# Square sums on VectorE, the statistics' product one tick later, first FFN output unit k-major, preparation DMAs on GpSimd's queue

## The chip, the cores and the metric

The kernel runs on one core of one Trainium2 chip. The metric is the device time of one execution in microseconds (us); lower is better. PE is TensorE, DVE VectorE, ACT ScalarE, POOL GpSimd, SP SyncE; SP computes nothing here and issues DMAs. ACT and POOL issue DMAs too, each in order with its other instructions.

## What is computed

One step of a two-layer decoder on 576 tokens (512 of a prompt, 64 of samples), width 1024, fp32. Layer 0 mixes tokens with a gated MLP and differential attention, layer 1 with a diagonal state-space model (S5). Each mixer is followed by a normalised SwiGLU network. Cut to what the change touches:

```python
xp = xp + concat([a_p, b_p]) @ w_out_even[i]           # layer 0: output projection, residual
xp = xp + swiglu(rmsnorm(xp, norm_ffn[l]), w_ffn_in[l], w_ffn_out[l])
def rmsnorm(x, g): return x * lax.rsqrt(jnp.mean(x * x, axis=-1) + EPS) * g
def swiglu(h, w_in, w_out):
    gate, up = jnp.split(h @ w_in, 2, axis=-1)
    return (silu(gate) * up) @ w_out
# layer 1: S5, tables from a, dt, b, c, d only (they do not depend on x)
a_bar = jnp.exp(a * dt); b_bar = ((a_bar - 1.0) / a) * b
s = associative_scan(combine, (a_bar, b_bar @ u)) + a_cum * s0; y = Re(c @ s) + d * u
```

## The kernel before

**Layout.** The activations stay in SBUF as 8 feature blocks of 128 partitions by 576 tokens. A matrix product is cut into units: 128 output features, all tokens in two column halves of 288. fp32 precision comes from splitting each operand into a high and a low part (`hi`, `lo` for activations, `wh`, `wl` for weights) and adding three products (L278), so a unit over 8 input blocks takes 48 matmuls, one over 6 takes 36.

**The weight stream.** `Stream` holds all units in order. A `raw` tile (two units of weights) is loaded on SP's queue (L245); ACT copies it to `wh` (L260), DVE, or POOL for early units, subtracts to get `wl` (L263). `raw`, `wh` and `wl` have two buffers each, the matmuls four PSUM banks. A unit's evacuation runs on DVE. In a normal unit the first half's products over all input blocks come first, then the second half's; with `kmajor=True` the first of the two units of a push takes both halves input block by input block (`unit_mm`).

**Statistics.** `Stat` sums the squares of the residual stream over the 8 blocks: ACT squares a block (L980, L983), POOL adds it to `acc` (L991), and for the last block the square stays apart (`last`). Two sets of five tiny matmuls with a vector of ones (L1000, five column blocks of tokens) reduce `acc` and `last` over the partitions into `ssq`; twelve small DVE operations make the reciprocal root, and `bcast_rows` spreads it (`rb`). The division by the norm is applied when the FFN's first product is evacuated (L1104, L1114). There are three: `st1` after the output projection (evacuation `ev_o`, L1040), `st2` after layer 0's FFN (`ev_x2`, its products are L1518), `st3` after layer 1's mixer (`ev_z1`).

**FFN.** `push_ffn` handles the 22 blocks of hidden features in parts of 6, 6, 6 and 4: for each hidden block a gate and an up unit, then 8 output units over that part's blocks. `tu` times `tg` (L1116) gives the hidden block; ACT makes its `hi` (L227), DVE its `lo` (L228).

**S5 preparation.** Side work is split into generators; a `Driver` advances them a tick at a time between groups of matmuls. `s5_prep` builds the S5 tables during layer 0's FFN: it loads parameters (`ast`, `s0st`, `dq`, `braw`, `cst`), computes on DVE and ACT into tiles of two pools (`ablk`, 19 buffers, and `op`, 5 buffers for `Fn`, `Gn`), and stores through DRAM (`dF`, `dG`, `dZ`, `dL`, `dT`); `s5_load` loads the finished blocks back for layer 1 (`Gk`, `Fk`, `Tk`, `tabk`).

**Order.** The program is written as one sequence; a scheduler then fixes, ahead of the run, the order of instructions on every engine and DMA queue. Each engine runs its list strictly in order.

Of the kernel before, what the change touches and what calls it, by code (L numbers as in the profile page):

```python
# [77 lines left out]
def kernel(ctx, tc, I, O, stop=None, dbg=None):  # L78
# [1170 lines left out]
    def s5_prep():  # L1249
        ast = ablk("ast", (64, 4, P))  # L1250
        for c in range(2):
            A.dma_start(out=ast[:, 0, 64 * c:64 * c + 64], in_=I["ssm_a_re"][0])
            A.dma_start(out=ast[:, 1, 64 * c:64 * c + 64], in_=I["ssm_a_im"][0])
        A.dma_start(out=ast[:, 3, 0:1], in_=I["ssm_log_dt"][0].unsqueeze(1))
        V.tensor_copy(ast[:, 2, :], ast[:, 3, 0:1].to_broadcast([64, P]))
        s0st = ablk("s0st", (P, 4, P))
# [198 lines left out]
        for k in range(KD):  # L1455
# [472 lines left out]
```

## Time and profile before

| | |
|---|---|
| Median of 3 runs | 1450.46 us (1450.17 to 1450.61) |
| The profiled execution's own time | 1450.84 us |
| Its span, first to last instruction | 1449.1 us (1.7 us lie outside) |
| PE busy | 1392.5 us, 96% of the span |
| DVE, ACT, POOL busy | 829.9, 479.6, 232.8 us |
| Mean granted clock of TensorE | 0.984 |

The stages in the span: layer 0's input projection and mixers to about 340 us, its output projection to 380, its FFN to 840 (the preparation for S5 beside it), S5 to 910, layer 1's gated product and FFN from there to the end. Times of rows count from the span's start. In a row's bracket stands how long its engine was idle just before it, and what ended that.

### The profile page before, as it was taken

How to read it: one execution, taken by the hardware profiler on the slowest of the kernel's cores; microseconds unless marked ns; L12 is line 12 of the kernel's file. 1: busy time of each engine (PE TensorE's matmuls, PEld its weight loads, DVE VectorE, ACT ScalarE, POOL GpSimd, SP SyncE). 2: the span in 40 equal slices, each digit the busy share in tenths (PEclk: the TensorE clock that was granted, in tenths of full speed). 3: DMA queues.
4: the chain of work that ended last, by engine and by line, in shares of the span. 5: the costliest groups of instructions: out<-in, count | busy, mean ns of one | idle time of the engine just before them, and what ended most of it. 6: DMA issues, size and time to landing. Idle time of an engine off the chain costs nothing. (4 is left out here: it accounts for less than half of the span.)

```text
span 1449.1 us, 27653 instructions
## 1 busy us (share of the span) xinstructions
PE 1392.5 (96%) x11382; PEld 1316.6 (91%) x11382; DVE 829.9 (57%) x1955; ACT 479.6 (33%) x860; POOL 232.8 (16%) x250
## 2 busy tenths in 40 slices
PE   7999999988999999999999979999999999999997
PEld 6878777868899999999998978999999999999997
DVE  6433456557689744987983478544444444444455
ACT  4233455442422123233322345433222222222234
POOL 2565656552200000000000110010000000000002
PEclk9999999999999999999999989999999999999999
DMA  7566544353332433454457485233223322322411
GB/s 240 168 196 193 172 146 134 110 183 106 96 85 66 146 88 79 138 164 123 143 144 218 128 259 183 67 88 85 62 74 98 92 66 81 88 81 70 114 59 66
DMA packets 223557, 177.37 MB, mean 122 GB/s; under 512 B 34060, under 2 KB 199752, under 8 KB 223432
## 3 DMA queue, kind: packets, MB, share of 16 engines
q1 hardware_dynamic: 206312, 136.01, 32.4%
q0 software_dynamic: 10880, 35.66, 8.2%
q10 hardware_dynamic: 6240, 3.93, 0.9%
q8 instruction: 90, 1.47, 0.4%
q14 instruction: 35, 0.29, 0.1%
HBM read 154.24 MB, written 25.53 MB: 124 GB/s over the span
## 5 line engine op out<-in xcount | busy, mean ns | idle before, releaser
L278 PE MATMUL acc<-hi,wh 128*128 128x288 f32 x2432 | 724.3, 298 | 9.3 <-ACT wh L260 3.1
L278 PE MATMUL acc<-hi,wl 128*128 128x288 f32 x2432 | 719.3, 296 | 1.5 <-DVE wl L263 1.4
L278 PE MATMUL acc<-lo,wh 128*128 128x288 f32 x2432 | 718.7, 296 | 0.5 <-DVE lo L228 0.5
L278 PEld LDWEIGHTS acc<-hi,wh 128*128 128x128 f32 x2432 | 458.2, 189 | 16.6 <-ACT hi L227 4.9
L278 PEld LDWEIGHTS acc<-hi,wl 128*128 128x128 f32 x2432 | 458.6, 189 | 3.1 <-DVE wl L263 2.4
L278 PEld LDWEIGHTS acc<-lo,wh 128*128 128x128 f32 x2432 | 458.8, 189 | 1.8 <-issue 1.0
L260 ACT CAST wh<-raw 128x1024 fp32r<-128x1024 f32 (+2 forms) x196 | 184.9, 945 | 594.8 <-PE acc L278 405.8
L263 DVE TENSOR_TENSOR wl<-raw,wh 128x1024 fp32r<-128x1024 f32 (+2 forms) x173 | 191.7, 1108 | 52.6 <-ACT wh L260 51.9
L1114 DVE TENSOR_TENSOR tu<-acc,rb 128x288 f32<-128x288 f32 x88 | 40.1, 456 | 124.7 <-PE acc L278 124.6
L278 PE MATMUL acc<-gxh,wh 128*128 128x288 f32 x320 | 102.3, 323 | 0.9 <-DVE proj L372 0.9
L991 POOL TENSOR_TENSOR acc<-acc,sq 128x576 f32<-128x576 f32 x18 | 26.8, 1489 | 460.8 <-ACT sq L983 460.8
L278 PE MATMUL acc<-gxl,wh 128*128 128x288 f32 x320 | 97.3, 305 | 0.0
L278 PE MATMUL acc<-gxh,wl 128*128 128x288 f32 x320 | 96.5, 304 | 0.6 <-DVE wl L263 0.6
L1104 DVE TENSOR_TENSOR tg<-acc,rb 128x288 f32<-128x288 f32 x88 | 40.0, 456 | 97.2 <-PE acc L278 96.2
L1124 DVE TENSOR_TENSOR x<-acc,x 128x288 f32<-128x288 f32 x96 | 43.8, 457 | 73.4 <-PE acc L278 73.0
L1834 POOL TENSOR_TENSOR sq<-sq,sq 128x288 f32<-128x288 f32 x12 | 9.6, 803 | 431.2 <-ACT sq L1830 431.2
L725 POOL DMA_INDIRECT pg<-in_cache_k_dram,pidx x64 | 61.9, 966 | 61.0 <-PE ktp L780 24.6
L725 POOL DMA_INDIRECT pg<-in_cache_v_dram,pidx x64 | 64.3, 1004 | 44.1 <-PE so L847 14.0
L278 PEld LDWEIGHTS acc<-gxh,wh 128*128 128x128 f32 x320 | 61.8, 194 | 8.8 <-issue 8.1
L278 PEld LDWEIGHTS acc<-gxl,wh 128*128 128x128 f32 x320 | 62.2, 195 | 1.9 <-issue 1.6
L278 PEld LDWEIGHTS acc<-gxh,wl 128*128 128x128 f32 x320 | 61.5, 193 | 1.9 <-DVE wl L263 0.8
L263 POOL TENSOR_TENSOR wl<-raw,wh 128x1024 fp32r<-128x1024 f32 (+1 forms) x23 | 46.8, 2035 | 39.0 <-ACT wh L260 38.7
(441 smaller groups left out, 1522.6 us busy)
## 6 DMA issues: line engine op xcount, KB each, us to landing
raw<-in_w_ffn_in_dram SPq DMA_DIRECT2D x88, 512.0 KB
raw<-in_w_ffn_out_dram SPq DMA_DIRECT2D x24, 768.0 KB
raw<-in_w_in_even_dram SPq DMA_DIRECT2D x10, 1024.0 KB
raw<-in_w_glu_dram SPq DMA_DIRECT2D x16, 512.0 KB
raw<-in_w_out_even_dram SPq DMA_DIRECT2D x8, 512.0 KB
dF<-Fn SPq DMA_DIRECT2D x16, 256.0 KB
dG<-gt SPq DMA_DIRECT2D x16, 256.0 KB
dL<-dZ SPq DMA_DIRECT2D x64, 64.0 KB
```

Of the source, the lines that this page charges most:

```text
L260: c = A.copy(hi[:, 0:nk], src)
L263: c = (lo_eng or V).tensor_tensor(lo[:, 0:nk], src, f32(hi[:, 0:nk]), op=ALU.subtract)
L278: PE.matmul(pts[hf], lhsT=w[:, k, :], rhs=x[:, c0:c1], start=(k == 0 and wi == 0), stop=(k == nk - 1 and wi == 2))
L725: G.indirect_dma_start(out=t, out_offset=None, in_=src, in_offset=bass.IndirectOffsetOnAxis(ap=pidx[:, 8 * b + j:8 * b + j + 1], axis=0))
L991: G.tensor_tensor(self.acc[:, 0:NT], self.acc[:, 0:NT], q, op=ALU.add)
L1104: V.tensor_tensor(half(t, hf), pt, half(stat.need(), hf), op=ALU.mult)
L1114: V.tensor_tensor(half(t, hf), pt, half(stat.need(), hf), op=ALU.mult)
L1124: V.tensor_tensor(half(nxt[m], hf), pt, half(cur[m], hf), op=ALU.add)
L1834: G.tensor_tensor(acc[h], acc[h], q, op=ALU.add)
```

## The change

Five edits. (1) The sum of squares moves from POOL to DVE. (2) The product with `acc` is issued in `steps()` together with that of `last`, one tick of the driver later; the flag `pre` goes. (3) In `ev_o` and `ev_z1` the split into `hi` and `lo` comes ahead of the square. (4) The first output unit of each FFN part is k-major (not in the last part of layer 1, which uses `push_parts`). (5) The DMAs of `s5_prep` that were on ACT's and SP's queues, and `s5_load` for the first two blocks, are issued on POOL's queue. From the diff:

```diff
-        def add(self, x, pre=True):
+        def add(self, x):
...
                     self.last = q
-                    if pre:
-                        self.mm(self.acc, True)
...
-                    G.tensor_tensor(self.acc[:, 0:NT], self.acc[:, 0:NT], q, op=ALU.add)
+                    V.tensor_tensor(self.acc[:, 0:NT], self.acc[:, 0:NT], q, op=ALU.add)
...
         def steps(self):
             yield
+            self.mm(self.acc, True)
             r = self.tm()
...
+            gx1[m] = split(x1[m], g_ffn0[:, m:m + 1])
             st1.add(x1[m])
-            gx1[m] = split(x1[m], g_ffn0[:, m:m + 1])
...
-                    W.push(loads[mp], nf, hs, [ev(2 * mp), ev(2 * mp + 1)])
+                    W.push(loads[mp], nf, hs, [ev(2 * mp), ev(2 * mp + 1)], kmajor=(mp == 0))
...
-            A.dma_start(out=ast[:, 0, 64 * c:64 * c + 64], in_=I["ssm_a_re"][0])
+            G.dma_start(out=ast[:, 0, 64 * c:64 * c + 64], in_=I["ssm_a_re"][0])
...
-            A.dma_start(out=dZ[k].rearrange("g c n -> (g c) n")[:, 0:112], in_=zz)
+            G.dma_start(out=dZ[k].rearrange("g c n -> (g c) n")[:, 0:112], in_=zz)
...
-                SP.dma_start(out=br[64 * c:64 * c + 64], in_=I[key][0, 32 * hf:32 * hf + 32].rearrange("g p c -> p g c"))
+                G.dma_start(out=br[64 * c:64 * c + 64], in_=I[key][0, 32 * hf:32 * hf + 32].rearrange("g p c -> p g c"))
...
-            SP.dma_start(out=dG[k][:, 4 * hh:4 * hh + 4, :], in_=gt)
+            G.dma_start(out=dG[k][:, 4 * hh:4 * hh + 4, :], in_=gt)
...
     def s5_load(k):
+        Q = G if k < 2 else SP
...
-                SP.dma_start(out=ts[hf], in_=src[:, 4 * hf:4 * hf + 4, :])
+                Q.dma_start(out=ts[hf], in_=src[:, 4 * hf:4 * hf + 4, :])
```

The same replacement is made for `s0st`, `dq`, `cst`, the stores to `dF`, the stores of `kr` to `dZ`, the copies to `dL`, and `Fk`, `Tk`, `tabk` of the first two blocks. POOL's list grows from 255 to 339 instructions, SP's shrinks from 309 to 219, ACT's from 794 to 777 (a row that the listing merges counts once). Three places show what moves; the rows are in each engine's own order, and the line numbers of the changed kernel differ by one or two from L991 on.

**The output projection's second half.** DVE before, two blocks' evacuations (`x`), each followed by the weights' `wl` for a later unit and the block's `lo`:

```order
L1040 TENSOR_TENSOR x_4586<-acc_4573,xa_4263 128x36x8
L1040 TENSOR_TENSOR x_4586<-acc_4588,xa_4263 128x36x8
L263 TENSOR_TENSOR wl_4610<-raw_4527,wh_4609 128x512
L231 SCALAR_TENSOR_TENSOR lo_4606<-x_4586,gvec,hi_4605 128x576
L1040 TENSOR_TENSOR x_4626<-acc_4613,xa_4265 128x36x8
L1040 TENSOR_TENSOR x_4626<-acc_4628,xa_4265 128x36x8
L263 TENSOR_TENSOR wl_4650<-raw_4527,wh_4649 128x512
L231 SCALAR_TENSOR_TENSOR lo_4646<-x_4626,gvec,hi_4645 128x576
```

DVE now:

```order
L1039 TENSOR_TENSOR x_4586<-acc_4573,xa_4263 128x36x8
L1039 TENSOR_TENSOR x_4586<-acc_4588,xa_4263 128x36x8
L263 TENSOR_TENSOR wl_4610<-raw_4527,wh_4609 128x512
L231 SCALAR_TENSOR_TENSOR lo_4603<-x_4586,gvec,hi_4602 128x576
L989 TENSOR_TENSOR acc_316<-acc_316,sq_4606 128x576
L1039 TENSOR_TENSOR x_4626<-acc_4613,xa_4265 128x36x8
L1039 TENSOR_TENSOR x_4626<-acc_4628,xa_4265 128x36x8
L263 TENSOR_TENSOR wl_4650<-raw_4527,wh_4649 128x512
L231 SCALAR_TENSOR_TENSOR lo_4643<-x_4626,gvec,hi_4642 128x576
L989 TENSOR_TENSOR acc_316<-acc_316,sq_4646 128x576
```

The add to `acc` stands behind each block's `lo`. On PE, at the end of the projection, the list before goes from the last product of the projection to `ssq` from `acc`, then to the first FFN unit (`acc_4791`, `acc_4795` are its two PSUM halves):

```order
L278 MATMUL acc_4704<-lo_3111,wh_4649 128x288
L278 MATMUL acc_4704<-hi_3110,wl_4650 128x288
L997 MATMUL ssq_4720<-ones 64x1
L1000 MATMUL ssq_4720<-ones,acc_316 128x1
L1000 MATMUL ssq_4720<-ones,acc_316 64x1
L1000 MATMUL ssq_4720<-ones,acc_316 128x1 x3
L278 MATMUL acc_4791<-hi_4441,wh_4783 128x288
L278 MATMUL acc_4791<-lo_4442,wh_4783 128x288
```

and now, after 24 products of that unit:

```order
L278 MATMUL acc_4788<-hi_4562,wh_4776 128x288
L278 MATMUL acc_4788<-lo_4563,wh_4776 128x288
L278 MATMUL acc_4788<-hi_4562,wl_4777 128x288
L995 MATMUL ssq_4810<-ones 64x1
L998 MATMUL ssq_4810<-ones,acc_316 128x1
L998 MATMUL ssq_4810<-ones,acc_316 64x1
L998 MATMUL ssq_4810<-ones,acc_316 128x1 x3
L998 MATMUL ssq_4810<-ones,sq_4722 128x1
L998 MATMUL ssq_4810<-ones,sq_4722 64x1
L998 MATMUL ssq_4810<-ones,sq_4722 128x1 x3
L278 MATMUL acc_4784<-hi_4602,wh_4776 128x288
```

Both sets of `ssq` products stand together there; before, the set from `last` stood at that place alone.

**POOL at the end of attention.** `osq` and `OS` belong to the attention's head norm, `wl` to the output projection. POOL before:

```order
L871 TENSOR_TENSOR osq_4089<-OS_699 128x512
L874 TENSOR_TENSOR OS_699<-OS_699,sub_b 128x512
L263 TENSOR_TENSOR wl_4268<-raw_4003,wh_4267 128x512
L1261 MEMSET zz_5003 128x112
L667 TENSOR_TENSOR osq_4181<-o_3966 128x512
L263 TENSOR_TENSOR wl_4302<-raw_4229,wh_4301 128x512
L263 TENSOR_TENSOR wl_4338<-raw_4229,wh_4337 128x512
```

POOL now (rows of a repeated kind left out: three more `ast`, the zero block's memset, five more `dZ` ahead of the second `osq`, one `dZ` ahead of the last `wl`):

```order
L871 TENSOR_TENSOR osq_4089<-OS_699 128x512
L1251 DMA ast_4993<-in_ssm_a_re_dram 64x64
L874 TENSOR_TENSOR OS_699<-OS_699,sub_b 128x512
...
L1253 DMA ast_4993<-in_ssm_log_dt_dram 64x1
L263 TENSOR_TENSOR wl_4268<-raw_4003,wh_4267 128x512
L1257 DMA s0st_5000<-in_state_ssm_re_dram 128x4x64
L1257 DMA s0st_5000<-in_state_ssm_im_dram 128x4x64
...
L1262 DMA dZ_4740<-zz_5003 128x112
...
L667 TENSOR_TENSOR osq_4181<-o_3966 128x512
L1262 DMA dZ_4746<-zz_5003 128x112
L263 TENSOR_TENSOR wl_4302<-raw_4229,wh_4301 128x512
...
L263 TENSOR_TENSOR wl_4338<-raw_4229,wh_4337 128x512
```

Thirteen DMAs stand ahead of the second `osq` (L667), two more ahead of the last `wl`.

**Layer 0's last FFN part.** ACT before, where `hi` belongs to hidden blocks of that part and `wh` to the units behind them:

```order
L260 CAST wh_9334<-raw_9134 128x1024
L227 CAST hi_9330<-tu_9301 128x576
L1106 ACTIVATE tg_9363<-tg_9363 128x576
L227 CAST hi_9453<-tu_9424 128x576
L260 CAST wh_9395<-raw_9269 128x1024
L260 CAST wh_9489<-raw_9269 128x1024
```

ACT now:

```order
L260 CAST wh_9334<-raw_9104 128x1024
L227 CAST hi_9330<-tu_9301 128x576
L260 CAST wh_9395<-raw_9269 128x1024
L1105 ACTIVATE tg_9363<-tg_9363 128x576
L260 CAST wh_9457<-raw_9269 128x1024
L227 CAST hi_9453<-tu_9424 128x576
```

The copy of `raw_9269` (the gate and up weights of the third hidden block) stood behind `hi_9453` of the second block and now stands ahead of it.

## Rows read from the trace of the kernel before

**Rows 1.** The page, busy time by engine.

```profile
PE 1392.5 (96%) x11382; PEld 1316.6 (91%) x11382; DVE 829.9 (57%) x1955; ACT 479.6 (33%) x860; POOL 232.8 (16%) x250
```

**Rows 2.** Waits of PE: total us, times, longest us.

```profile
PE acc L278 <- ACT wh L260: 3.1, 1, 3.1
PE acc L278 <- ACT hi L227: 3.0, 2, 2.6
PE ssq L1000 <- POOL acc L991: 2.5, 1, 2.5
PE acc L278 <- DVE wl L263: 2.0, 4, 0.6
```

**Rows 3.** Windows: length, busy us by engine (count), PE clock, DMA share, GB/s.

```profile
375.00:400.00 25.00, 22.04 (x154) 21.18 (x153) 14.84 (x29) 9.33 (x13) 3.18 (x7) 0.93 0.30 85
450.00:475.00 25.00, 22.38 (x158) 22.14 (x156) 23.56 (x118) 5.57 (x7) 1.20 (x2) 0.93 0.26 86
475.00:500.00 25.00, 25.00 (x191) 25.00 (x190) 21.48 (x90) 4.20 (x6) 3.23 (x6) 1.00 0.43 138
570.00:785.00 215.00, 210.55 (x1654) 203.36 (x1652) 166.73 (x294) 66.81 (x113) 0.00 (x0) 1.00 0.55 150
775.00:800.00 25.00, 21.47 (x149) 21.01 (x148) 7.85 (x11) 4.89 (x6) 0.00 (x0) 0.93 0.70 207
```

**Rows 4.** Timeline of DVE, output projection: start, us, engine line operation, count.

```profile
357.67 0.82 DVE L231 SCALAR_TENSOR_TENSOR lo<-x,gvec,hi 128x576 fp32r<-128x576 f32 x1 [0.90 <-ACT hi L230]
370.76 1.28 DVE L1040 TENSOR_TENSOR x<-acc,xa 128x288 f32<-128x288 f32 x2
371.86 0.69 DVE L263 TENSOR_TENSOR wl<-raw,wh 128x512 fp32r<-128x512 f32 x1
373.45 1.48 DVE L231 SCALAR_TENSOR_TENSOR lo<-x,gvec,hi 128x576 fp32r<-128x576 f32 x1 [0.90 <-ACT hi L230]
374.86 1.28 DVE L1040 TENSOR_TENSOR x<-acc,xa 128x288 f32<-128x288 f32 x2
```

**Rows 5.** Timeline of ACT in the same stretch.

```profile
372.07 0.68 ACT L983 ACTIVATE sq<-x 128x576 f32<-128x576 f32 x1 [2.24 <-DVE x L1040]
372.66 0.76 ACT L230 ACTIVATE hi<-x,gvec 128x576 fp32r<-128x576 f32 x1
```

**Rows 6.** Timeline of POOL there, of POOL and PE at its end.

```profile
372.89 1.43 POOL L991 TENSOR_TENSOR acc<-acc,sq 128x576 f32<-128x576 f32 x1 [2.67 <-ACT sq L983]
381.07 1.46 POOL L991 TENSOR_TENSOR acc<-acc,sq 128x576 f32<-128x576 f32 x1 [2.65 <-ACT sq L983]
382.58 1.35 PE L1000 MATMUL ssq<-ones,acc 128*128 128x1 f32 x10 [2.48 <-POOL acc L991]
```

**Rows 7.** Timelines of DVE, ACT, PE where part 0's output begins.

```profile
467.84 0.45 DVE L1114 TENSOR_TENSOR tu<-acc,rb 128x288 f32<-128x288 f32 x1
469.20 0.67 ACT L227 CAST hi<-tu 128x576 fp32r<-128x576 f32 x1 [3.35 <-DVE tu L1116]
469.92 0.40 PE L278 MATMUL acc<-hi,wh 128*128 128x288 f32 x1 [2.62 <-ACT hi L227]
469.95 0.76 DVE L228 TENSOR_TENSOR lo<-tu,hi 128x576 fp32r<-128x576 f32 x1
```

**Rows 8.** Timeline of ACT in layer 0's last FFN part.

```profile
784.62 0.67 ACT L227 CAST hi<-tu 128x576 fp32r<-128x576 f32 x1 [6.53 <-DVE tu L1116]
785.20 1.99 ACT L260 CAST wh<-raw 128x1024 fp32r<-128x1024 f32 x2
```

**Rows 9.** Timeline of POOL at the end of attention.

```profile
333.83 1.27 POOL L263 TENSOR_TENSOR wl<-raw,wh 128x512 fp32r<-128x512 f32 x1 [1.37 <-ACT wh L260]
339.91 1.04 POOL L667 TENSOR_TENSOR osq<-o 128x512 f32<-128x512 f32 x1 [4.68 <-DVE o L663]
```

**Rows 10.** POOL's own DMAs: plain (ns min/median/max), indirect (busy us, mean ns).

```profile
L1369 POOL DMA_DIRECT2D dT<-tab x8: 542/542/627, 464.6 to 494.0; - x8
L725 POOL DMA_INDIRECT pg<-in_cache_k_dram,pidx x64 | 61.9, 966 | 61.0 <-PE ktp L780 24.6
```

More of the change, by code (lines that the diff above doesn't have):

```diff
@@ L1251, in s5_prep @@
         for c in range(2):
-            A.dma_start(out=ast[:, 0, 64 * c:64 * c + 64], in_=I["ssm_a_re"][0])
-            A.dma_start(out=ast[:, 1, 64 * c:64 * c + 64], in_=I["ssm_a_im"][0])
-        A.dma_start(out=ast[:, 3, 0:1], in_=I["ssm_log_dt"][0].unsqueeze(1))
+            G.dma_start(out=ast[:, 0, 64 * c:64 * c + 64], in_=I["ssm_a_re"][0])
+            G.dma_start(out=ast[:, 1, 64 * c:64 * c + 64], in_=I["ssm_a_im"][0])
+        G.dma_start(out=ast[:, 3, 0:1], in_=I["ssm_log_dt"][0].unsqueeze(1))
         V.tensor_copy(ast[:, 2, :], ast[:, 3, 0:1].to_broadcast([64, P]))
@@ L1257, in s5_prep @@
         for c, key in enumerate(("state_ssm_re", "state_ssm_im")):
-            A.dma_start(out=s0st[:, :, 64 * c:64 * c + 64],
+            G.dma_start(out=s0st[:, :, 64 * c:64 * c + 64],
                         in_=I[key][0].rearrange("b g p -> (b g) p").rearrange("(i r) p -> r i p", r=P))
@@ L1373, in load_bc @@
             for c, key in enumerate(("ssm_b_re", "ssm_b_im")):
-                SP.dma_start(out=br[64 * c:64 * c + 64], in_=I[key][0, 32 * hf:32 * hf + 32].rearrange("g p c -> p g c"))
+                G.dma_start(out=br[64 * c:64 * c + 64], in_=I[key][0, 32 * hf:32 * hf + 32].rearrange("g p c -> p g c"))
             cs_ = ablk("cst", (P, 4, P))
             for c, key in enumerate(("ssm_c_re", "ssm_c_im")):
-                SP.dma_start(out=cs_[:, :, 64 * c:64 * c + 64],
+                G.dma_start(out=cs_[:, :, 64 * c:64 * c + 64],
                              in_=I[key][0, 32 * hf:32 * hf + 32].rearrange("(k g) c p -> (g c) k p", k=4))
@@ L1382, in s5_prep @@
         for q in range(4):
-            A.dma_start(out=dq[32 * q:32 * q + 32],
+            G.dma_start(out=dq[32 * q:32 * q + 32],
                         in_=I["ssm_d"][0].rearrange("(k par pr c) -> pr k par c", k=8, par=2, pr=4)[q].partition_broadcast(32))
@@ L1431, in kernel_rows @@
             for q in range(4):
-                SP.dma_start(out=dZ[k].rearrange("(par pr) c n -> pr c par n", par=2)[q][:, :, 112:240], in_=kr[32 * q:32 * q + 16])
+                G.dma_start(out=dZ[k].rearrange("(par pr) c n -> pr c par n", par=2)[q][:, :, 112:240], in_=kr[32 * q:32 * q + 16])
             ready.append(k)
@@ L1440, in transposed @@
             A.copy(gt, tp.rearrange("p (g c) -> p g c", g=4))
-            SP.dma_start(out=dG[k][:, 4 * hh:4 * hh + 4, :], in_=gt)
+            G.dma_start(out=dG[k][:, 4 * hh:4 * hh + 4, :], in_=gt)
         def toeplitz(k):
             for t in range(8):
-                SP.dma_start(out=dL[k].rearrange("(c t) g n -> t c g n", t=8)[t],
+                G.dma_start(out=dL[k].rearrange("(c t) g n -> t c g n", t=8)[t],
                              in_=dZ[k][:, :, 16 * (7 - t):16 * (7 - t) + P].rearrange("g c n -> c g n"))
@@ L1489, in s5_prep @@
                 f = outer(Cx, Cy, gs, js, 9, PU[0], PU[1], "Fn")
-                SP.dma_start(out=dF[k][:, js, :], in_=f[:, :, 1:9, :].rearrange("p g d c -> p g (d c)"))
+                G.dma_start(out=dF[k][:, js, :], in_=f[:, :, 1:9, :].rearrange("p g d c -> p g (d c)"))
                 late.append((kernel_rows, (k, hh, f, Bx)))
@@ L1527, in ev_x2 @@
             return
-        st2.add(n, False)
+        st2.add(n)
         if m == KD - 1:
@@ L1565, in s5_load @@
             for pa in range(2):
-                SP.dma_start(out=fk[c][64 * pa:64 * pa + 64], in_=dF[k][64 * c:64 * c + 64, 4 * pa:4 * pa + 4, :])
+                Q.dma_start(out=fk[c][64 * pa:64 * pa + 64], in_=dF[k][64 * c:64 * c + 64, 4 * pa:4 * pa + 4, :])
         tk = pair(dL[k], "Tk")
@@ L1570, in s5_load @@
                 t = ablk("tabk", (P, 8, 64))
-                SP.dma_start(out=t.rearrange("p a n -> p (a n)"), in_=dT[k // 2][:, c, :])
+                Q.dma_start(out=t.rearrange("p a n -> p (a n)"), in_=dT[k // 2][:, c, :])
                 tabs[k // 2, c] = t
```

2 lines of the change are left out of this document (1 added, 1 removed).

## The prediction

> **What bounds the kernel now.** The busy times come first [rows 1]: PE works 96% of the span, DVE 57%. The profiled execution took 1450.84 us, 0.4 above the median shown, and 1.7 of it lie outside the span. PE idles for 1449.1 - 1392.5 = 56.6 us. At the full clock PE starts a product every 25/191 = 0.131 us [rows 3]. No edit removes products, so the time can only come from PE's waits, and from stretches in which its clock is granted at the lower of its two levels.
>
> The waits of PE [rows 2] say which of these the change can reach: 2.5 us in one wait for POOL's `acc`, 2.6 in one for ACT's `hi` (0.4 in another), 3.1 for ACT's `wh`, and 2.0 in four waits for DVE's `wl`, of which I take three (0.48, 0.48 and 0.47 us by a closer look at the timeline; the row bounds each by 0.6). The windows around the three long waits [rows 3] show a mean clock of 0.93 where the one between them shows 1.00: 7% of 25 us, about 1.75 us each, on top of the wait. So a wait of 2.5 us costs 4.2.
>
> **The change, part by part.**
>
> *The output projection and st1.* Eight blocks pass through DVE. A full turn took 374.86 - 370.76 = 4.10 us [rows 4]: two `x`, `wl`, an idle 0.90 for ACT's `hi`, and `lo` at 1.48. The same `lo` took 0.82 for the first block, when POOL was not adding; POOL's add (1.43 us, from 372.89 [rows 6]) covers the later ones. ACT's `hi` is late because the square (0.68) runs ahead of it [rows 5]. Now `hi` comes first: its 0.76 ends about 0.81 after the second `x`, `wl` hides in that, `lo` follows at its lone 0.82 (0.74 to the next start), then the add. No DVE add of this shape stands here; the nearest row is `lo` in the FFN, 128x576 with two SBUF operands, 0.76 [rows 7]. The turn becomes 1.28 + 0.81 + 0.74 + 0.76 = 3.6. The square ends 1.5 after `x`, just before the add wants it. Six blocks have an add, so the last `x` comes 6 x 0.5 = 3 us sooner. PE needs 24 x 0.131 = 3.1 a block, so DVE still sets the pace there, and the two 0.48 waits for `wl` shrink or go.
>
> Then PE waited 2.48 us for POOL's last add (381.07 to 382.53) before the ten `ssq` products of 1.35 us [rows 6]. Now 24 products of the first FFN unit stand in between, 3.1 us. POOL's last add started with its square, so that block's `x` ended near 380.3; 2.5 us sooner, plus `wl` (1.2), `lo` and the add, the sum is ready near 380.5. PE came to the products at 382.58 - 2.48 = 380.1; less 0.96, plus 3.1, it is now 382.2. What could be late next is the last square: last `x` at 380.3 + 4.1 - 3 = 381.4, plus 0.76 and 0.68 on ACT, 382.8, while PE comes to it at 382.2 + 1.35 = 383.6. The margin is 0.8 us. Sum: 2.48 + 0.96 + 1.75 of clock = **-5.2**. Bounds: with DVE turns of 3.85 the square is 1.5 later, PE waits 0.7 and keeps a `wl` wait, and if the clock falls all the same -2.3 is left; 0.5 more than the sum, a margin on the reading of the waits, is the other end.
>
> *st2 and st3.* The other twelve adds sit in stages in which no wait of PE for `acc` or for the evacuations is among those named above; DVE's other work covers none of PE's path there. The products of st2 need the last square too, which no edit brings forward; **0**, bounds -0.5 and +0.8 (one 0.76 add ahead of the last `x`, or gone from ahead of it).
>
> *k-major.* At the start of part 0's output PE wanted the last hidden block after 17 products (15 by the code, two pulled ahead by the scheduler). DVE had held its `tu` to 467.84, so `hi` ended at 469.87 and PE went on at 469.92 after 2.62 us; `lo` ended at 470.71 [rows 7]. DVE's order there is unchanged, so the block comes no sooner. Now 30 products stand ahead, 13 x 0.131 = 1.7 us more work: PE waits 2.62 - 1.7 = 0.9 for `hi`, then 0.7 for `lo`, which was hidden behind the other half before. Saved: 2.62 - 1.6 = 1.0, plus 1.75 if the clock stays up through two short waits, which I take: -2.8, and the 0.4 of [rows 2] at part 3: **-3.2** (bounds -0.9 and -4.8). The other five first units have no wait to lose; their evacuations come as a pair, at 0.45 each [rows 7], under the next unit's 24 products or more.
>
> *SP and ACT in layer 0's last part.* The 3.1 us wait is not for bytes: `wh` of the third block ran at 785.20 because it stood behind a `hi` that ended at 785.29, which itself had waited 6.53 us for DVE's product [rows 8]. In the new order it stands ahead of that `hi`, and SP, with the copies and loads of the preparation gone, can load its weights earlier. The wait, a `wl` wait of 0.47 behind it and the dip in the clock go: **-5.3** (bounds 0 and -5.3; a later weight load now queues behind `Gk` of the third S5 block, which needs buffers that POOL's last stores free).
>
> *POOL at the end of attention.* What ACT issued beside its work, POOL issues in line. The nearest rows are its plain DMAs, 0.54 us each, and its indirect ones, 0.97 [rows 10]. Thirteen stand ahead of the `osq` at 339.91. Before it POOL idled 4.68, and 1.37 ahead of the `wl` at 333.83 [rows 9]. At 0.54: 7.0 - 6.05 = 1.0 us late; at 0.97: 12.6 - 6.05 = 6.6. DVE's reduction waits for `osq`, and the projection's evacuations queue behind it, so PE pays nearly all. I take the plain row, a little more for the two `s0st` loads with their short runs: **+1.5** (bounds +1.0 and +6.6, plus 1.75 if the clock dips). ACT's own queue, then free, cost PE nothing.
>
> *The preparation.* From 570 to 785 POOL did nothing; DVE was busy 166.7 of 215 us, PE 210.6 [rows 3]. 136 transfers move there: 73 us at 0.54, 132 at 0.97. Both fit, and POOL no longer holds up SP's weight loads; **0**. The 18 loads of the first two S5 blocks have some 55 us until S5 starts: 0.
>
> Sum: -5.2 - 3.2 - 5.3 + 1.5 = -12.2, from 1450.84 to 1438.6; against the median **1438.3 us**.
>
> A rule speaks against edit 5; first the rows that bear on it. At 475 to 500 us DVE was busy 21.48 of 25 us [rows 3], and POOL's plain DMAs, all but two of them in that stretch, still took 0.54, at most 0.63 [rows 10]. The Trainium skill, "SBUF — State Buffer", section "SBUF: two separate sides", says that GpSimd can't write a transfer's descriptors while VectorE holds the SBUF ports that both share in its faster modes; "A bandwidth-pool intuition that's wrong" there gives about 620 ns for such a transfer alone and 3100 ns beside a copy. At 3.1 us the 136 would take an estimated 422 us. The rows here don't show it, but these operations may not be of the kind.
>
> **The rivals.**
> - *The clock still dips.* Short waits remain at two of the three places (for the last square, for `lo`, or for weights), enough for the clock to fall again. For: the k-major unit keeps two waits, the square has 0.8 us of margin. Against: every wait shrinks to a third or less. Two dips and 1 us of waiting: 1438.3 + 4.5 = 1442.8.
> - *POOL's DMAs are dear at the end of attention* (0.97 us, as indirect ones). For: short runs. Against: the plain row. 1438.3 + 6.6 - 1.5 + 1.75 = 1445.2.
> - *POOL can't keep up with the preparation.* `Fn` and `Gn` have five buffers; when their stores are late DVE waits for a buffer, and every evacuation behind it on DVE with it. It decides from a mean of 215/136 = 1.58 us per transfer, waits for its inputs included (each store waits in line for another engine's result). At 1.75 the preparation ends 23 us late: 1461. For: the `braw` loads have 16 times the runs of `dT`. Against: at 0.54 two thirds of POOL stay free.
> - *DVE locks POOL out.* POOL gets the 48 us in 215 that DVE leaves [rows 3], a 0.54 us transfer takes 0.54/0.22 = 2.4, 136 of them 330, so the preparation ends 115 us late: 1553. This is what the rule of the Trainium skill's "SBUF — State Buffer" would do here; [rows 10] speak against it.
>
> **How the numbers follow.** Forecast 0.55, dips 0.21, dear DMAs 0.09, POOL too slow 0.12, lock 0.03. Two runs of this kernel can be told apart from about 0.2%, 2.9 us. Faster by more: the first three cases, 0.85, less 0.05 for those in which small losses add up, 0.80; that 0.05 and a little of the fourth, the same, 0.06; slower the rest, 0.14. The likeliest case's own range, from its bounds, is 1434 to 1443. Most of its open ends are losses; leaving out some 0.05 below and 0.15 above gives 1432 to 1450.
>
> **What would show it.** Right: no wait of PE for `acc` at 380, `lo` at 0.82 throughout the projection and turns of 3.6; a mean clock of 1.00 where it was 0.93; two short waits instead of one at part 0; none at 786; a wait of DVE for `osq` near 342 longer by 1 us. Wrong: POOL's plain DMAs above 1 us, DVE waiting for a DMA of `Fn` between 570 and 785, PE waiting for `sq` in the first FFN unit.

## The result, and the profile after

The changed kernel took 1438.55 us (median of 4 runs, 1436.87 to 1440.30), the kernel before 1450.53 (4 runs, 1450.17 to 1451.69): ratio 0.9915, 95% interval 0.9903 to 0.9927, 12 us faster. The profiled execution took 1440.3 us, its span is 1438.6.

The page's busy times of the changed kernel, beside [rows 1]:

```profile
PE 1389.5 (97%) x11382; PEld 1316.7 (92%) x11382; DVE 833.8 (58%) x1973; ACT 479.8 (33%) x860; POOL 305.4 (21%) x405
```

PE's idle time fell from 56.6 to 1438.6 - 1389.5 = 49.1 us. PE's waits of before that touch the end of attention (one row), and those of the changed kernel that answer to [rows 2]:

```profile
PE acc L278 <- DVE xa L1033: 1.8, 1, 1.8
```

```profile
PE acc L278 <- DVE xa L1032: 4.4, 1, 4.4
...
PE acc L278 <- DVE wl L263: 0.9, 2, 0.6
...
PE acc L278 <- ACT hi L227: 0.7, 1, 0.7
```

The waits for POOL's `acc` (2.5) and ACT's `wh` (3.1) are gone, `hi` is down from 3.0 to 0.7, `wl` from 2.0 to 0.9. A wait that the prediction doesn't name has grown: `xa`, from 1.8 to 4.4. The windows follow as in [rows 3] (length, busy us by engine, clock, DMA share, GB/s). First the end of attention before, which [rows 3] doesn't have:

```profile
325.00:350.00 25.00, 20.29 (x175) 18.66 (x174) 21.28 (x72) 6.40 (x13) 8.61 (x8) 1.00 0.47 134
```

Then the changed kernel:

```profile
325.00:350.00 25.00, 19.11 (x153) 17.90 (x151) 20.36 (x63) 5.46 (x11) 15.73 (x22) 0.86 0.42 142
375.00:400.00 25.00, 24.73 (x175) 24.07 (x175) 17.66 (x36) 11.22 (x16) 0.00 (x0) 0.93 0.42 118
450.00:475.00 25.00, 23.84 (x178) 23.39 (x177) 24.93 (x127) 6.29 (x8) 1.14 (x2) 1.00 0.26 85
...
570.00:785.00 215.00, 213.37 (x1682) 206.96 (x1681) 169.84 (x298) 68.74 (x115) 85.18 (x150) 1.00 0.54 157
775.00:800.00 25.00, 25.00 (x191) 25.00 (x190) 11.15 (x16) 6.28 (x9) 0.86 (x2) 1.00 0.63 179
```

Two of the three places that showed 0.93 now show 1.00. The third, 375 to 400, still shows 0.93, though PE idles only 0.27 us there. And at the end of attention, 325 to 350, the clock went from 1.00 to 0.86.

**Where the time went, stage by stage.** All kernels send the same 8448 wide products (L278) to PE, so a count of them names the same place in each. The table takes the time between two counts in one kernel, less the same time before; times of the places are those of before. "Again" is the changed kernel's second profile (fifth run below).

| Stage (us, before) | predicted | after | again |
|---|---|---|---|
| start to 299, no edit | 0 | +2.2 | -5.5 |
| 299 to 358, end of attention | +1.5 | +3.5 | +5.3 |
| 358 to 401, projection and st1 | -5.2 | -4.2 | -5.6 |
| 465 to 482, part 0's first output unit | -2.8 | -2.7 | -2.6 |
| 533 to 777, preparation | 0 | -1.6 | -1.6 |
| 777 to 798, third hidden block's weights | -5.3 | -5.6 | -5.6 |
| 798 to 825, part 3's first output unit | -0.4 | -0.4 | -0.4 |
| 825 to 943, S5 | 0 | -0.8 | -0.7 |
| 943 to 1019, st3 | 0 | 0.0 | +1.5 |
| 1019 to 1431, layer 1's FFN | 0 | -0.8 | -0.6 |
| sum (rounded terms) | -12.2 | -10.4 | -15.8 |

The first row is not the change's: up to 299 us the instructions and their order are those of before, and over the runs below that row goes from -8.1 to +3.3. It goes with the series that a run belongs to: -0.5 to +3.3 where the kernel before took 1450 to 1453 us, -4.6 to -8.1 where it took about 1445. Without it the changed kernel gained 12.6 us in the one profile and 10.3 in the other. Stages left out show no difference.

The projection, timeline of DVE in the changed kernel, one turn from `x` to `x` (start, us, engine, line; in brackets the idle time ahead and what ended it):

```profile
367.42 1.28 DVE L1039 TENSOR_TENSOR x<-acc,xa 128x288 f32<-128x288 f32 x2
...
369.55 0.82 DVE L231 SCALAR_TENSOR_TENSOR lo<-x,gvec,hi 128x576 fp32r<-128x576 f32 x1 [0.33 <-ACT hi L230]
370.28 0.76 DVE L989 TENSOR_TENSOR acc<-acc,sq 128x576 f32<-128x576 f32 x1
370.95 1.32 DVE L1039 TENSOR_TENSOR x<-acc,xa 128x288 f32<-128x288 f32 x2
```

The turn is 370.95 - 367.42 = 3.53 us against 4.10 [rows 4], `lo` has its lone 0.82, the wait for `hi` fell from 0.90 to 0.33, and the add takes the 0.76 that the FFN's `lo` had suggested. PE of the changed kernel, at the statistics' products and at part 0's first output unit:

```profile
387.33 1.35 PE L998 MATMUL ssq<-ones,acc 128*128 128x1 f32 x10
388.54 1.33 PE L998 MATMUL ssq<-ones,sq 128*128 128x1 f32 x10
...
471.36 0.40 PE L278 MATMUL acc<-hi,wh 128*128 128x288 f32 x1 [0.73 <-ACT hi L227]
472.20 0.40 PE L278 MATMUL acc<-lo,wh 128*128 128x288 f32 x1 [0.44 <-DVE lo L228]
```

No wait stands ahead of either `ssq` set (2.48 before [rows 6]); a short one for `wl`, 0.27, has come up at the first FFN unit, 24 products ahead of them; the one wait of 2.62 [rows 7] became two of 0.73 and 0.44. ACT in layer 0's last part, beside [rows 8]:

```profile
774.10 1.05 ACT L260 CAST wh<-raw 128x1024 fp32r<-128x1024 f32 x1 [4.24 <-PE acc L278]
...
781.90 0.68 ACT L227 CAST hi<-tu 128x576 fp32r<-128x576 f32 x1 [0.39 <-DVE tu L1115]
```

The copy that PE had waited for, the first of the two behind `hi` in [rows 8], now runs 7.8 us ahead of that `hi`; the second, at 780.46, runs 1.4 us ahead of it. Groups of POOL's transfers (busy us, mean ns, then idle time ahead):

```profile
L1444 POOL DMA_DIRECT2D dL<-dZ x64 | 34.2, 540 | 16.5 <-DMA dZ<-kr 13.5 <-issue 2.4 <-DMA Gk<-dG 0.4
...
L1489 POOL DMA_DIRECT2D dF<-Fn x16 | 12.4, 777 | 130.7 <-DVE Fn L1411 130.7
...
L1373 POOL DMA_DIRECT2D braw<-in_ssm_b_re_dram x2 | 2.2, 1120 | 0.0
```

Most cost what the plain row of [rows 10] said; only the four `braw` loads pass 1 us. So one of the prediction's signs of being wrong, a transfer above 1 us, came for these four. Before `Fn`'s stores POOL idles 130.7 us: it waits for DVE, not DVE for it.

**The end of attention.** DVE before, from the head norm's reduction to the first `xa` that PE waits for:

```profile
331.13 0.69 DVE L873 TENSOR_REDUCE oss<-osq 128x4 f32<-128x512 f32 x1 [0.45 <-POOL osq L871]
331.86 0.63 DVE L186 TENSOR_SCALAR var<-oss 128x4 f32<-128x4 f32 x1
...
332.72 0.17 DVE L173 TENSOR_SCALAR rsi<-rsi 128x4 int32<-128x4 int32 x1
...
333.80 0.45 DVE L1033 TENSOR_TENSOR xa<-acc,xa 128x288 f32<-128x288 f32 x1
```

DVE in the changed kernel:

```profile
333.06 0.69 DVE L873 TENSOR_REDUCE oss<-osq 128x4 f32<-128x512 f32 x1 [0.45 <-POOL osq L871]
333.78 1.13 DVE L186 TENSOR_SCALAR var<-oss 128x4 f32<-128x4 f32 x1
334.94 0.17 DVE L172 TENSOR_SCALAR rsi<-var 128x4 int32<-128x4 int32 x1
335.15 1.24 DVE L173 TENSOR_SCALAR rsi<-rsi 128x4 int32<-128x4 int32 x1
336.42 0.16 DVE L177 TENSOR_TENSOR rst<-rsi 128x4 f32<-128x4 f32 x1
...
337.01 1.22 DVE L177 TENSOR_TENSOR rst<-rsy 128x4 f32<-128x4 f32 x1
...
338.34 0.45 DVE L1032 TENSOR_TENSOR xa<-acc,xa 128x288 f32<-128x288 f32 x1
```

and POOL there:

```profile
332.96 0.59 POOL L1251 DMA_DIRECT2D ast<-in_ssm_a_re_dram  x1
333.57 1.30 POOL L874 TENSOR_TENSOR OS<-OS,sub_b 128x512 f32<-128x512 f32 x1
...
335.87 0.53 POOL L1252 DMA_DIRECT2D ast<-in_ssm_a_im_dram  x1
...
336.91 1.29 POOL L263 TENSOR_TENSOR wl<-raw,wh 128x512 fp32r<-128x512 f32 x1
...
345.84 1.04 POOL L667 TENSOR_TENSOR osq<-o 128x512 f32<-128x512 f32 x1 [2.44 <-DVE o L663]
```

From the reduction to `xa` it is 338.34 - 333.06 = 5.28 us, before 2.67. Three operations on 128x4, 0.16 to 0.17 us where nothing holds them, make the difference: L186 ends at 334.91 as POOL's `OS` ends (334.87), L173 at 336.39 as the fourth `ast` transfer ends (336.40), the second L177 at 338.23 as POOL's `wl` ends (338.20); 0.50 + 1.07 + 1.06 = 2.63 over before. (L186 took 0.63 before: it ran beside `OS` then too.) And the second `osq` (L667) was not late by POOL's list: POOL waited 2.44 us for DVE ahead of it, and DVE's reduction behind it waited 0.42 us for it, where it had waited 0.70 before.

### The profile page after: what moved, and what is told of

Read it like the earlier page. It is cut to its first block, busy times and chain, and to the rows that moved or that the text cites. A ratio compares the mean times of both kernels' runs of the same rounds, so it can differ in the third digit from the quotient of the medians.

```text
span 1438.6 us, 27649 instructions
## 1 busy us (share of the span) xinstructions
PE 1389.5 (97%) x11382; PEld 1316.7 (92%) x11382; DVE 833.8 (58%) x1973; ACT 479.8 (33%) x860; POOL 305.4 (21%) x405
## 4 chain that ended last, share of the span: by engine, by line
PE 83%; DVE 9%; DMA 2%; ACT 2%; issue 2%; POOL 1%; SPq 0%; another core or an unknown queue 0%; POOLq 0%; ACTq 0%; DVEq 0%
PE acc L278 70%; PE ktp L780 2%; PE ssc L761 2%; DVE wl L263 1%; PE yp L1702 1%; PE S L632 1%; PE so L847 1%; DMA Gk<-dG 1%; PE satp L821 1%; PE yp L1696 1%; DMA xt<-in_x_sample_dram 1%; PE gT L1437 1%; PE O L661 0%; PE vp L1639 0%; DMA U<-dU 0%
## 5 line engine op out<-in xcount | busy, mean ns | idle before, releaser
L278 PE MATMUL acc<-hi,wh 128*128 128x288 f32 x2432 | 723.9, 298 | 6.6 <-DVE xa L1032 4.4
L278 PE MATMUL acc<-lo,wh 128*128 128x288 f32 x2432 | 718.6, 296 | 0.9 <-DVE lo L228 0.9
L278 PE MATMUL acc<-hi,wl 128*128 128x288 f32 x2432 | 718.9, 296 | 0.3 <-DVE wl L263 0.3
L278 PEld LDWEIGHTS acc<-hi,wh 128*128 128x128 f32 x2432 | 458.0, 188 | 12.8 <-DVE xa L1032 4.7
L278 PEld LDWEIGHTS acc<-lo,wh 128*128 128x128 f32 x2432 | 458.4, 189 | 2.2 <-DVE lo L228 1.4
L278 PEld LDWEIGHTS acc<-hi,wl 128*128 128x128 f32 x2432 | 458.2, 188 | 0.7 <-DVE wl L263 0.5
L278 PE MATMUL acc<-gxh,wh 128*128 128x288 f32 x320 | 102.1, 322 | 0.9 <-DVE proj L372 0.9
L278 PE MATMUL acc<-gxl,wh 128*128 128x288 f32 x320 | 97.3, 305 | 0.0
L278 PE MATMUL acc<-gxh,wl 128*128 128x288 f32 x320 | 96.5, 304 | 0.6 <-DVE wl L263 0.6
L278 PEld LDWEIGHTS acc<-gxh,wh 128*128 128x128 f32 x320 | 61.9, 194 | 8.9 <-issue 8.1
L278 PEld LDWEIGHTS acc<-gxl,wh 128*128 128x128 f32 x320 | 62.0, 194 | 1.9 <-issue 1.6
L278 PEld LDWEIGHTS acc<-gxh,wl 128*128 128x128 f32 x320 | 61.5, 193 | 1.9 <-DVE wl L263 0.8
L785 DVE COPY kt<-ktp 128x512 f32<-128x512 f32 x32 | 22.0, 689 | 42.8 <-PE ktp L780 40.5
```

The source lines that it names most:

```text
L278: PE.matmul(pts[hf], lhsT=w[:, k, :], rhs=x[:, c0:c1], start=(k == 0 and wi == 0), stop=(k == nk - 1 and wi == 2))
L785: V.tensor_copy(kt, tp)
```

## The experiments

Ratios are to the kernel before, on the same chip and in the same series, with 95% intervals; stages are read as in the table. The first four runs are one series (the kernel before: 1452.81 us), the fifth to eighth the second (1444.71), then two of two (1445.25 and 1451.61). So times of different series can't be set side by side, nor with a time that an expectation took from another series; ratios and stages (but for the first row) can. A ratio need not equal the quotient of the two medians: here they differ by up to 0.002.

**Why `xa` is late.** Theory L: DVE's small operations are held while POOL works or issues. Theory Q, the prediction's: POOL's list delays its own products. The first run puts the `ast` and `s0st` loads back on ACT, the second only the zeroing of `dZ`.

```diff
-            G.dma_start(out=ast[:, 0, 64 * c:64 * c + 64], in_=I["ssm_a_re"][0])
+            A.dma_start(out=ast[:, 0, 64 * c:64 * c + 64], in_=I["ssm_a_re"][0])
...
-            G.dma_start(out=s0st[:, :, 64 * c:64 * c + 64],
+            A.dma_start(out=s0st[:, :, 64 * c:64 * c + 64],
```

> The changed kernel with the seven loads of ast and s0st back on ACT's queue; the zeroing of dZ (eight transfers) stays on POOL. The stretch from the end of attention to the first product of the FFN lost 3.5 us of PE time in the changed kernel. Theory L (VectorE's small operations of the head norm are held while POOL works, and the ast transfers, which run beside them, hold them longer and push POOL's next wl onto them): PE's wait for xa goes back from 4.4 to about 1.8 us, the low clock after it goes, DVE's reduction and reciprocal-root steps there take at most about 1 us each once, and the time falls by 3 to 4 us against the changed kernel (1434.5 to 1435.5). Rival Q (POOL's list is late because each transfer takes its turn, as the prediction had it): seven of fifteen transfers gone give about half, 1.5 to 2 us, and POOL's osq is still 2 us late through the eight dZ.

```diff
-            G.dma_start(out=dZ[k].rearrange("g c n -> (g c) n")[:, 0:112], in_=zz)
+            A.dma_start(out=dZ[k].rearrange("g c n -> (g c) n")[:, 0:112], in_=zz)
```

> The changed kernel with only the zeroing of dZ (eight transfers) back on ACT's queue; ast and s0st stay on POOL. Theory L: these transfers come after the small operations of the first head norm; nothing comes back, PE waits 4.4 us for xa as before, the time stays within 1 us of the changed kernel (1438.5). Rival Q: six of the thirteen transfers ahead of osq are gone, 3.2 us of POOL's list; 1.5 to 2 us come back.

First run: 1438.12 us, 0.9896 (0.9878 to 0.9914); the wait for `xa` is 1.8 again and the stage costs +0.2. Second: 1441.95, 0.9931 (0.9913 to 0.9949); the wait stays at 4.5, the stage at +2.7. DVE in the first:

```profile
332.52 0.69 DVE L873 TENSOR_REDUCE oss<-osq 128x4 f32<-128x512 f32 x1 [0.44 <-POOL osq L871]
...
334.12 0.17 DVE L173 TENSOR_SCALAR rsi<-rsi 128x4 int32<-128x4 int32 x1
...
335.19 0.45 DVE L1032 TENSOR_TENSOR xa<-acc,xa 128x288 f32<-128x288 f32 x1
335.55 1.09 DVE L180 SCALAR_TENSOR_TENSOR rsy<-rst,rsy 128x4 f32<-128x4 f32 x1
```

335.19 - 332.52 = 2.67, as before; one small operation is still held (L180, 1.09, beside POOL's `wl`), behind the first `xa`. So the five `ast` transfers beside the norm's chain cost, by the operations that they hold and by pushing `OS` and `wl` onto the chain's later ones; the two of `s0st`, which went back with them, had started behind it (338.11). The zeroing stores, six of the thirteen transfers ahead of `osq`, cost the wait nothing. Theory L holds, by the wait: it is 4.4 to 4.5 us in all ten profiles with these loads on POOL and 1.8 in all three without. The stage's time says less, +2.3 to +6.3 with them and +0.2, +1.9 and +0.2 without. In whole time the first run stands 3.8 us below the second, but its interval overlaps the changed kernel's of the result.

**k-major.** Third run, edit 4 undone:

```diff
-                    W.push(loads[mp], nf, hs, [ev(2 * mp), ev(2 * mp + 1)], kmajor=(mp == 0))
+                    W.push(loads[mp], nf, hs, [ev(2 * mp), ev(2 * mp + 1)])
```

> The changed kernel with edit 4 undone. Theory (the prediction's): at the start of part 0's output one wait of 2.6 us for hi and a low clock of 3.4 us after it come back, and the other parts change nothing: 2.7 to 3.2 us slower than the changed kernel, 1441.3 to 1441.7. Rival: the later driver ticks that k-major units have bring the gain (the side work is stepped differently), then the loss is spread over the parts and the wait at part 0 stays short.

1445.35 us, 0.9953 (0.9936 to 0.9970). One wait of 2.53 for `hi` is back, beside 2.62 before:

```profile
468.54 0.40 PE L278 MATMUL acc<-hi,wh 128*128 128x288 f32 x1 [2.53 <-ACT hi L227]
```

But the clock of 450 to 475 stays at 1.00 in this profile, so the stage is at -1.6, not 0. The k-major order is worth the other 1.0 to 1.1 us, in waiting. That it keeps the clock up is not shown, since the clock stayed up without it; the profiled execution (1442.29 us) is the second fastest of eight, and the median stands 3 us above it, so the others may have lost more. Part 3's first output unit (798 to 825) keeps its -0.4 without k-major, so that gain comes from another edit. Layer 1's FFN gains 0.1 instead of 0.8: the first units there, priced at nothing, gain too. The preparation gains 0.3 instead of 1.6, but it does no better in the seventh run, which has edit 4.

**Layer 0's last part.** Theory A: ACT's order made the 5.6 us. Theory B: SP's shorter list did. The fourth run gives SP the loads of the first two S5 blocks back, the tenth these and the copies to `dL`; ACT's order there stays the new one. The ninth gives SP all that it had had; with that ACT's list there has the order of before.

```diff
-        Q = G if k < 2 else SP
+        Q = SP
```

> The changed kernel with the loads of the first two S5 blocks back on SP's queue, between the last weight loads of layer 0. ACT's list keeps the changed kernel's order (wh of the third hidden block ahead of the second block's hi). Theory A (the wait of 3.1 us in layer 0's last part came from ACT's order): it stays away, the time is the changed kernel's within 1 us. Rival B (it came from SP's queue being full, so that weights landed late): the wait comes back, with the low clock behind it, 4 to 5 us slower, about 1443.

```diff
-            G.dma_start(out=dG[k][:, 4 * hh:4 * hh + 4, :], in_=gt)
+            SP.dma_start(out=dG[k][:, 4 * hh:4 * hh + 4, :], in_=gt)
```

The ninth run makes this replacement for `braw`, `cst`, `kr`, `dG`, `dF`, `dL` and the loads:

> The changed kernel with every transfer that came from SP (B, C, the stores of kr, Gn, Fn, the copies to dL, the loads of the first two S5 blocks) back on SP's queue; the fifteen that came from ACT stay on POOL. With that the order of ACT's list in layer 0's last part is again that of before: the copy of the third hidden block's weights stands behind hi of the second. Theory A (ACT's order made the gain of 5.6 us there): PE waits about 3 us for wh again, the clock falls behind it, the stretch from 777 to 798 us costs as much as before (0 instead of -5.6), and the kernel is about 5.6 us slower than the changed one: ratio to before 0.994 to 0.996. Theory B (what SP fetches earlier made it): the same, so this run alone doesn't tell A from B; e10 beside it does. Theory C (neither; the gain is a later stage's slack): the stretch stays at -5.6, ratio 0.990.

> The changed kernel with the 64 copies to dL and the loads of the first two S5 blocks back on SP's queue, so SP again holds 82 of the 90 transfers that it had lost more of; ACT's order in layer 0's last part stays that of the changed kernel (the copy of the third hidden block's weights ahead of hi of the second). Theory A (ACT's order): no wait of PE for wh over 0.5 us there, the stretch from 777 to 798 us stays at -5.6 us, ratio to before 0.990. Theory B (SP's shorter list): SP is late with the raw weights again, ACT's copy waits for them, PE waits some 3 us, the stretch comes to about 0, ratio 0.994 to 0.996.

Fourth: 1442.08 us, 0.9923 (0.9905 to 0.9940), stage -5.6. Tenth: 1432.14, 0.9916 (0.9900 to 0.9933), stage -5.6. Ninth: 1438.34, 0.9943 (0.9921 to 0.9965), stage +0.7. ACT, then PE in the ninth run:

```profile
774.71 0.67 ACT L227 CAST hi<-tu 128x576 fp32r<-128x576 f32 x1 [6.54 <-DVE tu L1115]
775.28 1.99 ACT L260 CAST wh<-raw 128x1024 fp32r<-128x1024 f32 x2
```

```profile
776.38 0.61 PE L278 MATMUL acc<-hi,wh 128*128 128x288 f32 x1 [3.06 <-ACT wh L260]
776.78 0.44 PE L278 MATMUL acc<-lo,wh 128*128 128x288 f32 x1
```

With the old order the old wait is there again, 3.06 us, and PE goes on at the lower clock (products of 0.44). With the new order it is gone even where SP carries 82 of its 90 moved transfers. Theory A holds. Why the order written for ACT turns on queues of other engines is the scheduler's doing, and was not taken apart.

**st1, edit by edit.** The fifth run repeats the changed kernel. The sixth undoes edit 2 (for `st1` and `st3`), the seventh edit 1.

> The changed kernel once more, unaltered, as the reference of this series on this chip. The stretches that no run's edit touches should show how much of a difference between two profiles is not the kernel's: up to 3 us before 330 us. The low clock behind the twenty small products at st1 and st3 comes by the theory of chance in some executions and not in others (so far in 3 of 5 profiles at st1, 4 of 5 at st3).

```diff
                     self.last = q
+                    if not self.fast:
+                        self.mm(self.acc, True)
...
-            self.mm(self.acc, True)
             r = self.tm()
```

> The changed kernel with edit 2 undone: the product with acc is issued again as soon as the last square is made, for st1 and st3. Theory (the prediction's, that the later tick hides the wait for the sum): PE waits 1 to 1.5 us for VectorE's last add at the end of the output projection; st1 costs 1 to 1.5 us more than in the changed kernel. At st3 nothing waits. Rival (what edit 2 gives in waiting it takes back in clock, since twenty one-column products in a row are followed by a low clock): at st3 the low clock of 3.4 to 6.8 us after the products is gone, 1.3 to 2.8 us, and the sum is 0 or slightly faster than the changed kernel.

```diff
-                    V.tensor_tensor(self.acc[:, 0:NT], self.acc[:, 0:NT], q, op=ALU.add)
+                    G.tensor_tensor(self.acc[:, 0:NT], self.acc[:, 0:NT], q, op=ALU.add)
```

> The changed kernel with edit 1 undone: the squares are summed on POOL, with the split still ahead of the square and the product still late. Theory (the prediction's: POOL's add holds VectorE's lo, 1.48 us instead of 0.82): with the square now behind hi, the add starts about 0.76 us later and falls beside the next x, whose first operand is in PSUM; lo takes 0.82, VectorE's turn is about 3.2 to 3.5, and the last add ends near 386; the time is within 1 us of the changed kernel, or up to 1 us better. Rival: POOL's add still lies beside lo or holds x or wl, turns stay above 4 us, PE waits for acc after the 24 products, 1.5 to 3 us slower.

Fifth: 1433.27 us, 0.9904 (0.9881 to 0.9927). Sixth: 1434.76, 0.9930 (0.9905 to 0.9955); PE waits 0.9 for `acc`. Seventh: 1433.61, 0.9905 (0.9880 to 0.9929), no wait for `acc`. DVE, then POOL in the seventh:

```profile
367.86 0.82 DVE L231 SCALAR_TENSOR_TENSOR lo<-x,gvec,hi 128x576 fp32r<-128x576 f32 x1 [0.33 <-ACT hi L230]
368.60 1.61 DVE L1039 TENSOR_TENSOR x<-acc,xa 128x288 f32<-128x288 f32 x2
```

```profile
368.55 1.42 POOL L989 TENSOR_TENSOR acc<-acc,sq 128x576 f32<-128x576 f32 x1 [1.73 <-ACT sq L983]
```

The add on POOL falls beside `x` now, not beside `lo`: `lo` keeps 0.82, `x` takes 1.61 instead of 1.28, and `x` follows `x` after 3.2 us instead of 3.5. So with edits 2 and 3 in place edit 1 brings nothing that can be measured; the stage from 358 to 401 stands at -6.2 without it, at -5.6 in the fifth run. The later product (edit 2) takes the last 0.9 us of wait. That the split ahead of the square (edit 3) is what frees `lo` is argued from the seventh run; no run undoes edit 3.

**The clock at st1 and st3.** Edit 2 puts twenty products of one column in a row. First run, PE at st3:

```profile
997.95 1.35 PE L998 MATMUL ssq<-ones,acc 128*128 128x1 f32 x10
999.16 1.33 PE L998 MATMUL ssq<-ones,sq 128*128 128x1 f32 x10
...
1001.62 0.29 PE L278 MATMUL acc<-hi,wh 128*128 128x288 f32 x1
1001.75 0.37 PE L278 MATMUL acc<-lo,wh 128*128 128x288 f32 x1
...
1002.16 0.44 PE L278 MATMUL acc<-hi,wh 128*128 128x288 f32 x1
1002.40 0.44 PE L278 MATMUL acc<-lo,wh 128*128 128x288 f32 x1
```

PE waits for nothing here; yet from 1001.92 its products start 0.24 us apart instead of 0.13, the lower of its two levels (1.2 GHz). The eighth run has the first run's loads on ACT and st3's set from `acc` early, as before. The eleventh sets one more tick, twelve wide products, between the two sets in both statistics, the twelfth in `st1` of the eighth's version.

```diff
             self.mm(self.acc, True)
+            yield
             r = self.tm()
```

> The changed kernel with the loads of ast and s0st back on ACT's queue and the product with acc early for st3 alone (late for st1). By the runs so far the first is worth 3.2 us of PE time at the end of attention. If the low clock at st3 comes from the twenty small products in a row, it stays away here and the kernel is another 1.5 us faster on average: 1433 to 1435, faster than the changed kernel. If it comes by chance wherever the products stand, the gain is the 3 us alone.

> The changed kernel with one more tick of the driver between the ten products with acc and the ten with the last square, in st1 and in st3: twelve wide products of the FFN's first unit stand between the two sets, and the root and its spread over the partitions come twelve products later. Theory R (twenty one-column products in a row bring the clock down): no low clock behind them, st1's stretch 380 to 401 us at about -3.5 us beside before and st3's at 0, in every profile. Theory P (the place in the first FFN unit, or chance, brings it down, not the row of twenty): low clock at st3 again (+1.5 to +3.1), as in eight of nine profiles. Third case: the evacuation of the first gate unit now waits for the norm and PE for a PSUM bank, 1 to 2 us at 395. By R the ratio to before is 0.988 to 0.990, by P 0.990 to 0.992.

> The version of the eighth run (loads of ast and s0st on ACT, st3's product with acc early) with one more tick between the two sets of products in st1 alone. Theory R: no low clock at st1, its stretch at -3.5 us where the eighth run had -1.9, st3 at 0; ratio to before 0.986 to 0.988. Theory P: low clock at st1 in about six profiles of ten, and the ratio that the eighth run had, 0.9876. In either case the end of attention stays at +0.2 to +2 us, since DVE's small operations there no longer stand beside POOL's transfers.

Eighth: 1428.03 us, 0.9876 (0.9854 to 0.9898). Eleventh: 1437.69, 0.9903 (0.9886 to 0.9919). Twelfth: 1435.05, 0.9882 (0.9865 to 0.9898). Eleventh, windows at st1 and st3:

```profile
375.00:400.00 25.00, 24.49 (x183) 23.61 (x182) 17.59 (x36) 11.40 (x16) 0.00 (x0) 1.00 0.42 116
...
985.00:1010.00 25.00, 24.80 (x187) 24.17 (x186) 12.07 (x26) 8.97 (x13) 0.00 (x0) 1.00 0.31 85
```

Over all profiles: with twenty in a row the clock fell behind them in 6 of 10 at st1 and 8 of 9 at st3; with the sets apart in 0 of 3 at st1 (sixth, eleventh, twelfth; before, whose long wait stood there, is left out) and 0 of 5 at st3. A fall costs 1.5 us (from 380 to 401, st1's part of the row in the table: -3.5 without, -2.0 with), at st3 1.5, sometimes 3. Theory R holds at st3; st1's own count (6 of 10 against 0 of 3) would not decide it, and why the clock stayed up there behind four rows of twenty is open. In time it decides little: the eleventh run has that part at -3.0 and st3 at +0.4, the twelfth can't be told from the eighth. The eighth and the twelfth are the fastest versions; the eighth stands 5.2 us below the changed kernel of its series, with intervals that overlap.

## Why the prediction was right, and where its steps were not

- *Output projection and st1, -5.2: right in its mechanism, 1.0 too large in the first profile.* Turns of 3.53 (3.6 foreseen), `lo` at 0.82, no wait for `acc` or the last square. What is missing is the clock: the 1.75 was taken to hang on the wait, and the wait went while the fall stayed, behind the twenty small products. Where it didn't fall, the stage gave -5.6. The step let the clock fall behind a wait alone; here it also fell behind the row of small products. Two sizes are off as well, and offset each other. Up to the projection's last product the gain was 2.2, not 0.96: around each of the two waits for `wl` PE had lost 0.9 us, not the 0.48 in the bracket. From there to 401 it was 3.5 without the fall and 2.0 with it, not 2.48 + 1.75 = 4.2: a fall costs 1.5, and the new wait for `wl` takes some of the rest.
- *That edit 1 makes the shorter turn: not so.* The turn of 3.6 was built on the add in DVE's list; with the add on POOL behind the split, turns are 3.2.
- *st2 and st3, 0:* bounds -0.5 and +0.8; at st3 most profiles of this product order show +1.5 or +3, from the clock, which the term didn't consider.
- *k-major, -3.2: right in number (-2.7 and -0.4), in its mechanism for the waiting alone.* Waits of 0.73 and 0.44 stand where 0.9 and 0.7 were foreseen, worth the 1.0 of the sum. The 1.75 for the clock came to 1.5, but in the third run it came without k-major, and so did part 3's 0.4. "No wait to lose" for the other first units was 0.7 short in layer 1, by the third run.
- *SP and ACT, -5.3: right,* -5.6 in every kernel with the new ACT order, 0.7 without. Its side clause, that SP's shorter list matters, is neither needed nor borne out.
- *POOL at the end of attention, +1.5: wrong in its mechanism, and 2.0 too small.* The failed step is "DVE's reduction waits for `osq`": POOL had time to spare there, and that wait shrank from 0.70 to 0.42. What waited was the norm's chain on DVE, eight us earlier, whose small operations ended with POOL's; 2.6 us of waiting and 0.9 that is left to the clock.
- *Preparation, 0:* -1.6. POOL kept up (85 us busy of 215), no `Fn` buffer was waited for; the gain shrinks under unlike edits (0.8 to 0.9 with copies back on SP, 0.3 without k-major, 0.2 with the add on POOL, where PE waits 2.2 us for a `cst` load), and what makes it stays open.

The total, 1438.3 against 1438.55, is closer than its terms, and that is luck in part: st1 and attention came out 1.0 and 2.0 worse than foreseen, the preparation, S5 and layer 1's FFN 1.6, 0.8 and 0.8 better, and the first 299 us of that profile lost 2.2 that no edit made.

Of the rivals, *the clock still dips* came half true, at the place where the wait was gone and not at the one with two. *POOL's DMAs are dear* did not: they took 0.5 to 0.8 us at the end of attention. *DVE locks POOL out* did not happen: 64 copies at 0.54 us beside a DVE 79% busy. Here POOL held DVE. The Trainium skill, "SBUF — State Buffer", section "Who interferes with whom", says that a DVE instruction with two inputs from SBUF, or in a two-port mode, and a GpSimd instruction that reads SBUF exclude each other, and that the later one waits to the other's end. The row of the second L177, a product of two SBUF tiles, which ends within 0.04 us of POOL's `wl`, agrees; so does that of L186 beside `OS`, if its one input was read in such a mode, which no row shows. That a transfer's issue on GpSimd can hold a DVE operation (L173) the section doesn't say, and the short L172 and L177 beside other `ast` transfers show that not each does.

## What to carry to other kernels

Before transfers go to an engine's own list, look at what the other engines do beside them in that stretch, not only at what stands behind them in the list: five transfers of 0.55 us cost 2.6 us through three tiny operations of a critical chain, and 136 beside bulk work cost nothing that the table shows. When a change of queues moves time in a far stage, compare the engines' order there first; here two swapped ACT instructions were worth 5.6 us. And price a lost clock apart from the wait that it stands behind, since taking the wait away need not bring the clock back.

## What the runs showed of the hardware

- DVE operations on 128x4 took 1.1 to 1.2 us instead of 0.16 beside POOL's products and one of its transfers, and ended with them within 0.04 us; two beside other transfers kept 0.16 and 0.17.
- TensorE's clock fell to its lower level with no wait above 0.4 us in the 40 products ahead: behind twenty one-column products in a row in 14 of 19 cases, behind two sets of ten with at least twelve wide products between them in 0 of 8. Behind a wait of 2.53 us it stayed up once (third run), where it fell behind 2.62 before.
- POOL issued 64 copies at 0.54 us each beside a busy DVE; `braw`, with short runs, took 1.12, `s0st` 0.8.
